# Block 1's RWKV-7 recurrence: products of one head on 64 or 32 partitions in place of masked products over 128

## The chip, the cores and the metric

The kernel runs on one core of a Trainium2 chip. The core has a matrix engine (TensorE, PE in the profile; PEld is its loading of weights), a vector engine (VectorE, DVE), a scalar engine (ScalarE, ACT), GpSimd (POOL), and SyncE (SP), which here only starts transfers. The metric is the device time of one execution in microseconds, the median of the runs; lower is better.

## The reference

Two transformer blocks over one sequence of 512 tokens with 1024 channels. In the first, half of the channels go through dilated attention and half through a bidirectional RWKV-7 mixer, then a product-key expert layer follows; the second block has a hybrid mixer and a mixture of experts. The change concerns the scan of RWKV-7, eight heads of 64 channels, in both directions:

```python
def wkv7_scan(r, w, k, v, kk, a, reverse):
    state0 = jnp.zeros((B, H, N, N), jnp.float32)
    def step(state, inp):
        r_t, w_t, k_t, v_t, kk_t, a_t = inp
        sa = jnp.einsum('bhvk,bhk->bhv', state, -kk_t)
        state = (state * w_t[:, :, None, :]
                 + sa[..., :, None] * (kk_t * a_t)[..., None, :]
                 + v_t[..., :, None] * k_t[..., None, :])
        y = jnp.einsum('bhvk,bhk->bhv', state, r_t)
        return state, y
    _, ys = lax.scan(step, state0, xs, reverse=reverse)
```

## The kernel before

The scan is computed in chunks: 512 tokens are eight chunks of 64, and a state is handed only from chunk to chunk. Two heads of 64 channels form a pair (four pairs, `j`), and a pair has two directions (`dr`). All of it is the function `rwkv`.

For each pair and direction, `elementwise` makes 128x512 operands with the channels of both heads on the partitions: `ar` (two of them), `x` (name `bx`), `y` (`kx`) and the decay `cum`. `by_head` makes from them `bd`: copies in which the other head's partitions are zeroed by the mask `own`, so that a product over all 128 partitions is that of one head. `within` transposes four operands to tokens-on-partitions (`transposed`, L611; the second direction's `vt` is instead turned by products with `flip`, L666), multiplies within each chunk (`pa` L694, then `pvy` and `pq`, L704 to L708, through masked `kbd`), and so gets the triangular matrices of each chunk. Tokens of two chunks lie on the 128 partitions here, so `vb` is again a masked copy.

`invert` and `solve` invert each chunk's triangular matrix: blocks of 16 by elimination, then blocks of 32 and 64 by small products, `p1` (L744 to L753) and `p2` (L764 to L770; the profile calls both `p`), whose operands `X`, `Z` (`Zb`), `V` (`Vb`) and `W` (`Wb`) are spread with zeros so that a product over 128 partitions is right. Then `pm` (L780), its two masked copies `M` (L783), and `pr`, `pq2` (L790 to L796) give per chunk `PB`, `RP` and `QQ`. `chain` walks the chunks: two sets of products into `pS` (L872, L875), four updates of the state `Sb` per chunk (L880), each of 64x64. `finish` normalises the pair's output (`mps`, L889).

The pairs are staged against each other: the loop over `j` does `forward` (`elementwise`, `within`) of pair `j` in the same turn as `backward` (`solve`), `invert`, `chain` and `finish` of pair `j - 1`. Between these, `fill` puts slices of the attention (`sps`, `ptps`, `po`) and of the modulation's products (`adaps`, L214, whose weights `adaw` stream in through two buffers of 512 KB). The recurrence is emitted at high priority. The order on each engine is set by the framework's scheduler from these priorities and its own estimate of times, not by the order of the text. After the last pair the output projection (`zps`) and the residual end block 1.

Of the kernel before, what the change touches and what calls it, by code (L numbers as in the profile page):

```python
# [40 lines left out]
def shape_consts():  # L41
# [15 lines left out]
    own = (p[:, None] // 64 == np.arange(2)[None, :]).astype(f)  # L57
    c["own"] = own
# [3 lines left out]
    i = np.arange(6)[None, :]  # L62
    c["m_b"] = np.concatenate([p[:, None] // 16 == np.arange(8), p[:, None] // 16 == i % 3 + 4 * (i // 3)], axis=1).astype(f)
    c["m_k"] = np.stack([r < q, r <= q], axis=1).astype(f)[:, :, None, :] * own[:, None, :, None]
# [14 lines left out]
    c["flip"] = np.eye(128, dtype=f)[::-1]  # L79
# [440 lines left out]
def rwkv(s, c, P, zrd, mixd, kkd, sad, gd, room, fill, tail):  # L520
# [23 lines left out]
    if True:  # L544
# [3 lines left out]
        gup = wp.tile([128, 512], F32, name="gup", tag="X", bufs=1)  # L548
        with tc.issue_after(s.ada_load.ins):
            own, m_nt, m_rb, m_e, m_b, m_k, id64, rst = [s.const(n, kp) for n in ("own", "m_nt", "m_rb", "m_e", "m_b", "m_k", "id64", "rst64")]  # L550
            for o, i in ((flip, A["k_flip"]), (lora, A["lora"]), (gup, A["g_up"])):
                nc.sync.dma_start(o, i)
# [8 lines left out]

        Zb = [kp.tile([128, 8, 2, 64], F32, name=f"Zb{d}") for d in range(2)]
        Vb = [kp.tile([128, 8, 4, 16], F32, name=f"Vb{d}") for d in range(2)]
        Wb = [kp.tile([128, 8, 2, 32], F32, name=f"Wb{d}") for d in range(2)]
        Sb = [kp.tile([128, 2, 2, 64], F32, name=f"Sb{d}") for d in range(2)]
        for t in Vb + Wb + Sb:
            nc.gpsimd.memset(t, 0.0)
# [49 lines left out]
        def elementwise(h, dr):  # L617
# [23 lines left out]
            x = wp.tile([128, 512], F32, name="bx", bufs=1)  # L641
            nc.gpsimd.tensor_tensor(x, rev(kkn), a, OP.mult)
            y = wp.tile([128, 512], F32, name="kx", bufs=1)
# [12 lines left out]

        def within(h, dr, ar, bd, x, y):
# [3 lines left out]
            if dr == 0:  # L661
                ps = transposed(h.zv)
            else:
                ps = P.tile([128, 4, 128], F32, name="tps", tag="tr")
                for tt in range(4):
                    mm(ps[:, tt, :], lhsT=flip, rhs=h.vt[:, 3 - tt, :], start=True, stop=True)  # L666
            h.vt = vt = wp.tile([128, 4, 128], F32, name="vt")
            nc.scalar.activation(vt, ps, AF.Copy)
            vb = wp.tile([128, 4, 2, 128], F32, name="vb", bufs=1)
            for cc in range(2):  # L670
                nc.scalar.activation(vb[:, :, cc, :], ps, AF.Copy, scale=own[:, cc:cc + 1])
            ta = wp.tile([128, 4, 2, 2, 64], F32, name="ta", bufs=3)
            ps = transposed(ar[:, 0, :])
            nc.scalar.activation(ta[:, :, :, 0, :], ps.rearrange("p a (e f) -> p a e f", e=2), AF.Copy)
            tb = wp.tile([128, 4, 2, 2, 64], F32, name="tb", bufs=3)
            ps = transposed(x)
            nc.scalar.activation(tb[:, :, :, 1, :], ps.rearrange("p a (e f) -> p a e f", e=2), AF.Copy)
            tk = wp.tile([128, 4, 128], F32, name="tk", bufs=1)
            ps = transposed(y)
            nc.scalar.activation(tk, ps, AF.Copy)  # L680
# [3 lines left out]
            for t2 in range(2):  # L684
                pv = P.tile([128, 2, 2, 2, 64], F32, name="pvy", tag="mm")
                pq = P.tile([128, 2, 2, 64], F32, name="pq", tag="mm")
                for ti in range(2):
                    tt = 2 * t2 + ti
# [7 lines left out]
                    nc.vector.tensor_tensor(db[:, 2 * tt:2 * tt + 2, :], pa[:, 0, :, 0, :], m_nt[:, None, :].to_broadcast([128, 2, 64]), OP.mult)  # L696
                    nc.vector.tensor_tensor(E[:, 2 * tt:2 * tt + 2, :], pa[:, 0, :, 0, :], m_e[:, None, :].to_broadcast([128, 2, 64]), OP.mult)
                    nc.vector.tensor_tensor(tb[:, tt, :, 0, :], pa[:, 0, :, 1, :], m_rb[:, None, :].to_broadcast([128, 2, 64]), OP.mult)
                    kb = wp.tile([128, 2, 2, 2, 64], F32, name="kbd")
                    for e in range(2):  # L700
                        nc.vector.tensor_tensor(kb[:, e], pa[:, 1, e, :, None, :].to_broadcast([128, 2, 2, 64]), m_k, OP.mult)
                    for cc in range(2):
                        for e in range(2):
                            mm(pv[64 * cc:64 * cc + 64, 0, ti, e, :], lhsT=kb[:, e, 0, cc, :], rhs=vt[:, tt, 64 * e:64 * e + 64], start=True, stop=True)  # L704
                    for e in range(2):
                        es = slice(64 * e, 64 * e + 64)
                        mm(pv[es, 1, ti, :, :], lhsT=vt[:, tt, es], rhs=kb[:, e, 1, :, :], start=True, stop=True)
                        mm(pq[es, ti, :, :], lhsT=tk[:, tt, es], rhs=vb[:, tt, :, es], start=True, stop=True)  # L708
                nc.scalar.activation(ta[:, 2 * t2:2 * t2 + 2, :, 1, :], pv[:, 0], AF.Copy)
                yv = yview(yacc, dr)[:, 256 * t2:256 * t2 + 256]  # L710
                py = pv[:, 1].rearrange("p a c t -> p (a c t)")
# [4 lines left out]
                nc.scalar.activation(QQ[:, dr, 4 * t2:4 * t2 + 4, :], pq.rearrange("p a c t -> p (a c) t"), AF.Copy)  # L716
# [9 lines left out]
        def solve(j, dr, held, zd, xd, QQ, PB, RP, y):  # L726
# [5 lines left out]
            for i, src in ((0, xd), (1, zd)):  # L732
                nc.sync.dma_start(zc[:, i], src[dr].rearrange("u g s t -> (g s) u t"))
            X = wp.tile([128, 8, 2, 3, 16], F32, name="X", bufs=1)
            nc.vector.tensor_tensor(X.rearrange("p u c q t -> p u (c q) t"), zc[:, 0, :, None, :].to_broadcast([128, 8, 6, 16]),
                                    m_b[:, None, 8:14, None].to_broadcast([128, 8, 6, 16]), OP.mult)
            nc.vector.tensor_tensor(Z.rearrange("p u c (q t) -> p u (c q) t", t=16), zc[:, 1, :, None, :].to_broadcast([128, 8, 8, 16]),
                                    m_b[:, None, 0:8, None].to_broadcast([128, 8, 8, 16]), OP.mult)

            p1 = P.tile([128, 3, 8, 16], F32, name="p1", tag="sv")  # L740
            for u in range(8):
                for g in range(4):
                    cc, h = g // 2, g % 2
                    mm(p1[32 * g:32 * g + 32, 0, u, :], lhsT=E[:, u, 32 * h:32 * h + 32], rhs=X[:, u, cc, 2 * h, :], start=True, stop=True)  # L744
            for g in range(4):
                po = slice(32 * g, 32 * g + 32)
                nc.scalar.activation(V[po, :, g, :], p1[po, 0], AF.Copy)
            for u in range(8):
                for g in range(4):
                    cc, h = g // 2, g % 2  # L750
                    mm(p1[32 * g:32 * g + 16, 1, u, :], lhsT=V[:, u, g, :], rhs=Z[:, u, cc, 32 * h + 16:32 * h + 32], start=True, stop=True)
                for cc in range(2):
                    mm(p1[64 * cc:64 * cc + 32, 2, u, :], lhsT=Z[:, u, cc, 0:32], rhs=V[:, u, 2 * cc, :], start=True, stop=True)  # L753
            for cc in range(2):
                po = slice(64 * cc, 64 * cc + 32)
                nc.vector.tensor_tensor(X[po, :, cc, 0, :], p1[po, 2], X[po, :, cc, 0, :], OP.add)
# [1430 lines left out]
```

## Time and profile before

| | |
|---|---|
| median of three runs | 2792.06 us (2790.89 to 2804.2) |
| profiled execution, its own time | 2790.26 us |
| its span, first to last instruction | 2788.5 us |
| mean granted TensorE clock | 0.961 |
| PE busy over the span | 2565.9 us (92%) |
| DVE, ACT, POOL busy | 1908.5, 1055.3, 1137.0 us |

Times are in microseconds from the span's start unless marked ns. "Busy" is time in which an engine executes; PE's weight loads lie beside its products. The recurrence's first product `pa` starts at 218 us, and block 1 ends at about 706 us; its output projection runs from 642 to 675 us with little else, and the chain of the last pair follows it, from 675 to 685 us. An f32 product on PE leaves two records, a transpose one. The tile of a product (as 128*64) is the rows and columns of the array that it uses; tiles of two column halves can run side by side.

### The profile page before, as it was taken

What the parts mean: (1) busy time and instruction counts of PE and PEld (TensorE: products, weight loads), DVE (VectorE), ACT (ScalarE), POOL (GpSimd) and SP (SyncE); (2) the same over time, 40 slices, a digit from 0 to 9 for tenths busy, and PEclk for the clock granted to TensorE, in tenths of its full rate; (3) what the DMA queues carried; (4) which work ended last, traced back from release to release, by engine and by line L of the source; (5) the groups of instructions that cost most, each with busy time, mean ns of one, the idle gap of its engine ahead of it and who ended that gap; (6) DMA issues with size and microseconds to landing.
All of it is one profiled execution on the core that took longest, in us unless ns stands there. A gap on an engine that the chain in (4) does not pass through costs nothing. (4 is left out here: it accounts for less than half of the span.)

```text
span 2788.5 us, 44586 instructions
## 1 busy us (share of the span) xinstructions
PE 2565.9 (92%) x16918; PEld 2037.5 (73%) x16918; DVE 1908.5 (68%) x3688; ACT 1055.3 (38%) x1973; POOL 1137.0 (41%) x864
## 2 busy tenths in 40 slices
PE   7999899978899997899999999999979999989995
PEld 4764455646789997899999999999967665654442
DVE  3666666743699888788888889888874377563323
ACT  3444344422434675233333333333333353222211
POOL 0012212111435766677767777776632123100002
PEclk9999999999999999999999999999989998889998
DMA  6527763371313678588888888886772212079984
GB/s 242 181 87 240 231 187 116 91 220 45 121 57 110 185 230 278 211 310 304 295 294 295 299 303 294 292 293 227 242 240 83 76 54 81 4 308 416 417 335 172
DMA packets 258888, 590.20 MB, mean 212 GB/s; under 512 B 48216, under 2 KB 121968, under 8 KB 248176
## 3 DMA queue, kind: packets, MB, share of 16 engines
q1 hardware_dynamic: 203584, 396.07, 41.1%
q0 software_dynamic: 38016, 138.43, 14.7%
q10 hardware_dynamic: 17072, 52.83, 5.1%
q8 instruction: 134, 2.20, 0.3%
q14 instruction: 82, 0.67, 0.1%
HBM read 530.23 MB, written 57.02 MB: 211 GB/s over the span
## 5 line engine op out<-in xcount | busy, mean ns | idle before, releaser
L165 PE MATMUL vacc<-gh,vhi 128*128 128x384 f32 x1024 | 347.0, 340 | 18.1 <-DVE xres L1359 9.9
L165 PE MATMUL ups<-phhi,uhi 128*128 128x384 f32 x1024 | 345.5, 338 | 6.0 <-ACT ge L1005 6.0
L167 PE MATMUL vacc<-gh,vlo 128*128 128x384 f32 x1024 | 324.0, 341 | 25.1 <-DVE vlo L171 20.0
L166 PE MATMUL ups<-phlo,uhi 128*128 128x384 f32 x1024 | 345.6, 338 | 1.3 <-DVE phlo L253 1.3
L166 PE MATMUL vacc<-gl,vhi 128*128 128x384 f32 x1024 | 346.0, 339 | 0.0
L167 PE MATMUL ups<-phhi,ulo 128*128 128x384 f32 x1024 | 345.4, 337 | 0.3 <-POOL ulo L171 0.3
L170 ACT ACTIVATE vhi<-vraw 128x512 fp32r<-128x512 f32 x256 | 161.0, 631 | 315.4 <-PE vacc L166 139.3
L171 POOL TENSOR_TENSOR vlo<-vraw,vhi 128x512 fp32r<-128x512 f32 x124 | 213.6, 1722 | 123.2 <-ACT vhi L170 105.3
L170 ACT ACTIVATE uhi<-uraw 128x1024 fp32r<-128x1024 f32 x128 | 135.6, 1060 | 284.8 <-PE ups L166 258.5
L1228 DVE SCALAR_TENSOR_TENSOR acc<-row,dot,acc 128x1024 f32<-128x1024 f32 x127 | 216.1, 1701 | 8.2 <-DMA row<-peer_v,peid 7.8
L167 PEld LDWEIGHTS vacc<-gh,vlo 128*128 128x128 f32 x1024 | 193.0, 192 | 30.5 <-DVE vlo L171 23.2
L165 PEld LDWEIGHTS vacc<-gh,vhi 128*128 128x128 f32 x1024 | 195.9, 192 | 20.8 <-DVE xres L1359 11.8
L1223 DVE CUSTOM_DVE_ANT_0 row<-row,phtok 128x1024 f32<-128x1024 f32 x128 | 195.1, 1525 | 10.7 <-DMA row<-u_rows,peid 10.7
L165 PEld LDWEIGHTS ups<-phhi,uhi 128*128 128x128 f32 x1024 | 193.5, 189 | 6.9 <-ACT ge L1005 6.7
L166 PEld LDWEIGHTS vacc<-gl,vhi 128*128 128x128 f32 x1024 | 195.8, 191 | 0.3
L166 PEld LDWEIGHTS ups<-phlo,uhi 128*128 128x128 f32 x1024 | 193.7, 189 | 1.7 <-DVE phlo L253 1.6
L167 PEld LDWEIGHTS ups<-phhi,ulo 128*128 128x128 f32 x1024 | 193.5, 189 | 0.9 <-POOL ulo L171 0.5
L1214 POOL DMA_INDIRECT row<-peer_v,peid x128 | 170.0, 1328 | 58.5 <-DVE acc L1228 33.4
L1214 POOL DMA_INDIRECT row<-u_rows,peid x128 | 167.7, 1311 | 50.8 <-DVE dot L1223 23.0
L171 DVE TENSOR_TENSOR vlo<-vraw,vhi 128x512 fp32r<-128x512 f32 x132 | 127.9, 970 | 73.5 <-ACT vhi L170 61.9
L1271 POOL TENSOR_TENSOR ge<-ge,wg 128x384 f32<-128x384 f32 x124 | 148.8, 1209 | 45.3 <-DMA wg<-wdr 31.7
L170 ACT ACTIVATE whi<-wraw 128x1024 fp32r<-128x1024 f32 (+1 forms) x81 | 84.7, 1046 | 209.4 <-PE zps L166 132.1
(655 smaller groups left out, 5719.0 us busy)
## 6 DMA issues: line engine op xcount, KB each, us to landing
uraw<-peer_u SPq DMA_DIRECT2D x128, 512.0 KB
vraw<-peer_v SPq DMA_DIRECT2D x256, 256.0 KB
wgu<-w_gu SPq DMA_DIRECT2D x32, 2048.0 KB
adaw<-ada_w SPq DMA_DIRECT2D x96, 512.0 KB
wdn<-w_dn SPq DMA_DIRECT2D x32, 1024.0 KB
wd<-wst SPq DMA_DIRECT2D x20, 1024.0 KB
wg<-wd ACTq DMA_DIRECT2D x16, 1280.0 KB
wraw<-w_in SPq DMA_DIRECT2D x22, 512.0 KB
```

Source lines behind the costliest of these rows:

```text
L165: mm(ps, lhsT=L[0], rhs=R[0], start=first, stop=False)
L166: mm(ps, lhsT=L[0], rhs=R[1], start=False, stop=False)
L167: mm(ps, lhsT=L[1], rhs=R[0], start=False, stop=last)
L170: s.nc.scalar.activation(hi, x, AF.Copy)
L171: return (eng or s.nc.vector).tensor_tensor(lo, x, hi.bitcast(F32), OP.subtract)
L1214: nc.gpsimd.indirect_dma_start(out=r, out_offset=None, in_=(urows, vrows)[which], in_offset=bass.IndirectOffsetOnAxis(ap=eid[:, p:p + 1], ...
L1223: nc.vector.tensor_tensor_reduce(out=r, in0=r, in1=htok, scale=1.0, scalar=0.0, op0=OP.mult, op1=OP.add, accum_out=dot[:, p:p + 1])
L1228: nc.vector.scalar_tensor_tensor(acc, r, dot[:, p:p + 1], acc, OP.mult, OP.add)
L1271: i = (nc.vector if grp == 0 and e % 2 == 0 else nc.gpsimd).tensor_tensor(g3, g3, W[0][:, :, e, :], OP.mult)
```

## The change

The same chunk of both heads now lies on the 128 partitions, in all stages of the recurrence: one head on rows 0 to 63 (`halves[0]`) and one on rows 64 to 127, or, where the matrices are inverted, four blocks of 32 (`quarters`). Every product is of one head alone, with its operands on 64 or 32 partitions and its result on the like. The masked copies `bd` and `vb`, the mask `own`, the second copy of `M`, the zeroed halves of `X`, `Z`, `V`, `W` and `Sb` and the `memset`s go. `x` and `y` are multiplied by `cum` on DVE, where POOL did it beside `bd`. `transposed` no longer uses PE's transpose of 128x128 but 16 ordinary f32 products of 64x64 with the identity as moving operand; `flip` turns within 64. The updates of `Sb` are two per chunk, over all 128 partitions.

```diff
         def transposed(src):
-            ps = P.tile([128, 4, 128], F32, name="tps", tag="tr")
-            for tt in range(4):
-                nc.tensor.transpose(ps[:, tt, :], src[:, 128 * tt:128 * tt + 128], s.ident)
+            ps = P.tile([128, 8, 64], F32, name="tps", tag="tr")
+            for ch in range(NCH):
+                for es in halves:
+                    mm(ps[es, ch, :], lhsT=src[es, 64 * ch:64 * ch + 64], rhs=s.ident[es, es], start=True, stop=True)
...
-            return ar, cum, x, y
-
-        def by_head(ar, cum, x, y):
-            bd = wp.tile([128, 2, 2, 512], F32, name="bd", bufs=1)
-            for i, z in ((0, x), (1, y)):
-                for e in range(2):
-                    nc.vector.scalar_tensor_tensor(bd[:, i, e, :], z, own[:, e:e + 1], cum, OP.mult, OP.mult)
-                nc.gpsimd.tensor_tensor(z, z, cum, OP.mult)
-            return ar, bd, x, y
+            nc.vector.tensor_tensor(x, x, cum, OP.mult)
+            nc.vector.tensor_tensor(y, y, cum, OP.mult)
+            return ar, x, y
...
-                    for i in range(2):
-                        for e in range(2):
-                            for cc in range(2):
-                                ch = 2 * tt + cc
-                                mm(pa[64 * cc:64 * cc + 64, i, e, :, :], lhsT=bd[:, i, e, 64 * ch:64 * ch + 64], rhs=ar[:, :, 64 * ch:64 * ch + 64],
-                                   start=True, stop=True)
+                    lo = 4 * t2 + 2 * ti
+                    for c in range(2):
+                        ts = slice(64 * (lo + c), 64 * (lo + c) + 64)
+                        for i, z in enumerate((x, y)):
+                            for es in halves:
+                                mm(pa[es, c, i, :, :], lhsT=z[es, ts], rhs=ar[es, :, ts], start=True, stop=True)
...
             for u in range(8):
-                for g in range(4):
-                    cc, h = g // 2, g % 2
-                    mm(p1[32 * g:32 * g + 16, 1, u, :], lhsT=V[:, u, g, :], rhs=Z[:, u, cc, 32 * h + 16:32 * h + 32], start=True, stop=True)
+                for g, gs in enumerate(quarters):
+                    h = g % 2
+                    mm(p1[32 * g:32 * g + 16, 1, u, :], lhsT=V[gs, u, :], rhs=Z[gs, u, 32 * h + 16:32 * h + 32], start=True, stop=True)
...
+            M = wp.tile([128, 8, 128], F32, name="M")
             for t2 in range(2):
...
-                M = wp.tile([128, 2, 2, 2, 128], F32, name="M")
-                for cc in range(2):
-                    nc.scalar.activation(M[:, :, :, cc, :], pm, AF.Copy, scale=own[:, cc:cc + 1])
+                nc.scalar.activation(M[:, cs], pm, AF.Copy)
...
                 if not last:
-                    for e in range(2):
-                        es = slice(64 * e, 64 * e + 64)
-                        for dr in range(2):
-                            nc.vector.scalar_tensor_tensor(Sn[es, dr, e, :], pS[es, 0, dr, :], GC[es, dr, ch:ch + 1], QQ[es, dr, ch, :], OP.mult, OP.add)
+                    for dr in range(2):
+                        nc.vector.scalar_tensor_tensor(Sn[:, dr, :], pS[:, 0, dr, :], GC[:, dr, ch:ch + 1], QQ[:, dr, ch, :], OP.mult, OP.add)
```

How this stands on PE, at two places. First, PE in the solve of pair 0's second direction, beside the forward products of pair 1's second direction; `p_...` is `p1`, and a row is a run of products with the shape of one. Before:

```order
L694 MATMUL pa<-ar,bd 64x128 x8
L704 MATMUL pvy<-vt,kbd 64x64 x3
L707 MATMUL pvy<-kbd,vt 64x128 x2
L751 MATMUL p_3052<-Zb_410,Vb_412 16x16 x4
L753 MATMUL p_3052<-Vb_412,Zb_410 32x16 x2
```

The changed program, at the same place:

```order
L736 MATMUL p_3233<-Vb_410,Zb_408 32x16 x2
L734 MATMUL p_3233<-Zb_408,Vb_410 16x16
L679 MATMUL pa<-ar,bx 64x128
L734 MATMUL p_3233<-Zb_408,Vb_410 16x16
L679 MATMUL pa<-ar,bx 64x128
L734 MATMUL p_3233<-Zb_408,Vb_410 16x16
L679 MATMUL pa<-ar,kx 64x128
L734 MATMUL p_3233<-Zb_408,Vb_410 16x16
L679 MATMUL pa<-ar,kx 64x128
L736 MATMUL p_3233<-Vb_410,Zb_408 32x16
```

Where eight `pa` stood together, single `pa` and single `p1` now alternate.

Second, PE in the second direction of pair 1, where its operands are transposed. Before:

```order
L780 MATMUL pm<-ta,Zb_409 64x128 x8
L214 MATMUL adaps<-adaw,crep_86 32x512 x2
L666 MATMUL tps<-vt,k_flip 128x128 x4
L611 MATMUL tps<-k_ident,ar 128x128 x4
L214 MATMUL adaps<-adaw,crep_86 32x512 x2
```

The changed program:

```order
L762 MATMUL pm<-ta,Zb_407 64x128 x8
L211 MATMUL adaps<-adaw,crep_86 32x512 x2
L657 MATMUL tps<-vt,k_flip 128x64 x8
L609 MATMUL tps<-k_ident,ar 64x64 x16
L769 MATMUL pr<-tb,M 64x128
L609 MATMUL tps<-k_ident,bx 64x64 x16
```

A set of four transposes has become one of 16 products, and a single `pr` now stands between two such sets.

## Rows read from the trace of the kernel before

**Rows 1.** Windows; columns: stretch, length, busy (x instructions), granted clock, DMA share, GB/s.

```profile
400.00:500.00 100.00, 86.89 (x1274) 55.32 (x1269) 67.27 (x209) 39.72 (x93) 20.25 (x17) 0.91 0.40 121
sum 506.00, PE 443.59 PEld 274.41 DVE 303.76 ACT 190.75 POOL 106.72; mean PE 88.72 PEld 54.88 DVE 60.75 ACT 38.15 POOL 21.34
```

**Rows 2.** Waits of PE, 200 to 706 us: us in total, times, longest.

```profile
PE adaps L214 <- DMA adaw<-ada_w: 31.0, 24, 3.5
PE lops L165 <- ACT mhi L170: 6.6, 1, 6.6
PE ptps L505 <- DVE pr L499: 5.2, 5, 3.1
PE pS L872 <- DVE Sb L880: 5.1, 9, 1.6
PE pa L694 <- DVE bd L653: 1.5, 4, 0.8
```

**Rows 3.** Groups by line, 200 to 706 us: xcount | busy us, mean ns | idle before.

```profile
L653 DVE SCALAR_TENSOR_TENSOR bd<-kx,k_own,cum 128x512 f32<-128x512 f32 x16 | 19.3, 1246 | 0.0
L653 DVE SCALAR_TENSOR_TENSOR bd<-bx,k_own,cum 128x512 f32<-128x512 f32 x16 | 12.5, 819 | 0.7 <-PE vps L167 0.7
L640 DVE TENSOR_TENSOR ar<-zr,ar 128x512 f32<-128x512 f32 x7 | 6.2, 892 | 1.0 <-ACT ar L637 1.0
L880 DVE SCALAR_TENSOR_TENSOR Sb<-pS,GC,QQ 64x64 f32<-64x64 f32 x96 | 23.0, 280 | 16.2 <-PE pS L875 15.5
L783 ACT ACTIVATE M<-pm,k_own 128x512 f32<-128x512 f32 x32 | 20.2, 684 | 30.7 <-PE pm L780 30.7
```

**Rows 4.** Timeline of PE: start us, us, what, xrecords, second turn's solve.

```profile
391.71 0.66 PE L790 MATMUL pr<-tb,M 128*64 128x128 f32 x8
392.20 0.39 PE L792 MATMUL pq<-M,tb 128*64 128x128 f32 x4
397.35 0.65 PE L611 MATMUL tps<-k_ident,bx 128*128 128x128 f32 x4
397.84 0.60 PE L611 MATMUL tps<-k_ident,kx 128*128 128x128 f32 x4
```

**Rows 5.** Timeline of PE, a long run of small products.

```profile
633.98 0.72 PE L744 MATMUL p<-X,E 128*32 128x16 f32 x56
```

**Rows 6.** Timeline of PE, single products of two shapes.

```profile
545.84 0.43 PE L694 MATMUL pa<-ar,bd 128*64 128x128 f32 x2
546.21 0.21 PE L751 MATMUL p<-Zb,Vb 128*16 128x16 f32 x2
546.35 0.43 PE L694 MATMUL pa<-ar,bd 128*64 128x128 f32 x2
```

**Rows 7.** Timeline of PE, the same beside `p2`.

```profile
557.90 0.33 PE L704 MATMUL pvy<-vt,kbd 128*64 128x64 f32 x2
558.16 0.26 PE L770 MATMUL p<-Zb,Wb 128*32 128x32 f32 x4
558.34 0.34 PE L704 MATMUL pvy<-vt,kbd 128*64 128x64 f32 x4
```

**Rows 8.** Timeline of PE, the last pair's chain.

```profile
674.97 0.46 PE L872 MATMUL pS<-Sb,PB 128*64 128x64 f32 x8
675.25 0.45 PE L875 MATMUL pS<-RP,Sb 128*64 128x64 f32 x8
676.07 0.99 PE L872 MATMUL pS<-Sb,PB 128*64 128x64 f32 x7 [0.37 <-DVE Sb L880]
677.72 0.99 PE L872 MATMUL pS<-Sb,PB 128*64 128x64 f32 x7 [0.37 <-DVE Sb L880]
```

**Rows 9.** Timeline of DVE, the last pair's chain.

```profile
675.75 0.99 DVE L880 SCALAR_TENSOR_TENSOR Sb<-pS,GC,QQ 64x64 f32<-64x64 f32 x4
```

**Rows 10.** Timeline of PE, block 2, two row halves.

```profile
2320.77 0.27 PE L1738 MATMUL gp<-SD,V 64*64 64x64 f32 x1
2320.78 0.27 PE L1742 MATMUL gp<-SD,V 64*64 64x64 f32 x1
```

More of the change, by code (lines that the diff above doesn't have):

```diff
@@ L560, in rwkv @@
         nc.vector.tensor_scalar(hwa, s.v("w0", 0, 16), 0.5, None, OP.mult)
[L562 to L567, printed above, removed]
+        Zb = [kp.tile([128, 8, 64], F32, name=f"Zb{d}") for d in range(2)]
+        Vb = [kp.tile([128, 8, 16], F32, name=f"Vb{d}") for d in range(2)]
+        Wb = [kp.tile([128, 8, 32], F32, name=f"Wb{d}") for d in range(2)]
+        Sb = [kp.tile([128, 2, 64], F32, name=f"Sb{d}") for d in range(2)]
+        halves = [slice(0, 64), slice(64, 128)]
+        quarters = [slice(32 * g, 32 * g + 32) for g in range(4)]
         def c64(x):
@@ L663, in within @@
             else:
[L664 to L667, printed above, removed]
+                ps = P.tile([128, 8, 64], F32, name="tps", tag="tr")
+                for ch in range(NCH):
+                    mm(ps[:, ch, :], lhsT=flip, rhs=h.vt[:, 7 - ch, :], start=True, stop=True)
+            h.vt = vt = wp.tile([128, 8, 64], F32, name="vt")
             nc.scalar.activation(vt, ps, AF.Copy)
-            vb = wp.tile([128, 4, 2, 128], F32, name="vb", bufs=1)
-            for cc in range(2):
[L671 to L680, printed above, removed]
+            ta = wp.tile([128, 8, 2, 64], F32, name="ta", bufs=3)
+            nc.scalar.activation(ta[:, :, 0, :], transposed(ar[:, 0, :]), AF.Copy)
+            tb = wp.tile([128, 8, 2, 64], F32, name="tb", bufs=3)
+            nc.scalar.activation(tb[:, :, 1, :], transposed(x), AF.Copy)
+            tk = wp.tile([128, 8, 64], F32, name="tk", bufs=1)
+            nc.scalar.activation(tk, transposed(y), AF.Copy)
             db = wp.tile([128, 8, 64], F32, name="db", bufs=1)
@@ new lines, in within @@
+                    for c in range(2):
+                        for es in halves:
+                            mm(pq[es, 2 * ti + c, :], lhsT=tk[es, lo + c, :], rhs=vt[es, lo + c, :], start=True, stop=True)
+                    for c in range(2):
+                        for es in halves:
+                            mm(pv[es, 0, 2 * ti + c, :], lhsT=kb[es, c, 0, :], rhs=vt[es, lo + c, :], start=True, stop=True)
+                    for c in range(2):
+                        for es in halves:
+                            mm(pv[es, 1, 2 * ti + c, :], lhsT=vt[es, lo + c, :], rhs=kb[es, c, 1, :], start=True, stop=True)
@@ L733, in solve @@
                 nc.sync.dma_start(zc[:, i], src[dr].rearrange("u g s t -> (g s) u t"))
[L734 to L738, printed above, removed]
+            X = wp.tile([128, 8, 3, 16], F32, name="X", bufs=2)
@@ L754, in solve @@
-            for cc in range(2):
-                po = slice(64 * cc, 64 * cc + 32)
-                nc.vector.tensor_tensor(X[po, :, cc, 0, :], p1[po, 2], X[po, :, cc, 0, :], OP.add)
-            for g in range(4):
-                po = slice(32 * g, 32 * g + 16)
-                nc.scalar.activation(Z[po, :, g // 2, 32 * (g % 2) + 16:32 * (g % 2) + 32], p1[po, 1], AF.Copy)
+                for g, gs in enumerate(quarters):
+                    h = g % 2
+                    mm(p1[gs, 0, u, :], lhsT=E[gs, u, 32 * h:32 * h + 32], rhs=X[gs, u, 2 * h, :], start=True, stop=True)
@@ new lines, in solve @@
+            nc.scalar.activation(V, p1[:, 0], AF.Copy)
+            for u in range(8):
+                for g, gs in enumerate(quarters):
+                    h = g % 2
+                    mm(p1[32 * g:32 * g + 16, 1, u, :], lhsT=V[gs, u, :], rhs=Z[gs, u, 32 * h + 16:32 * h + 32], start=True, stop=True)
+                for gs in quarters[::2]:
+                    mm(p1[gs, 2, u, :], lhsT=Z[gs, u, 0:32], rhs=V[gs, u, :], start=True, stop=True)
+            for gs in quarters[::2]:
+                nc.vector.tensor_tensor(X[gs, :, 0, :], p1[gs, 2], X[gs, :, 0, :], OP.add)
@@ new lines, in solve @@
+                    lo, hi = quarters[2 * cc:2 * cc + 2]
+                    mm(p2[lo, 1, u, :], lhsT=W[hi, u, :], rhs=Z[hi, u, 32:64], start=True, stop=True)
+            for lo in quarters[::2]:
+                nc.scalar.activation(Z[lo, :, 32:64], p2[lo, 1], AF.Copy)
+            M = wp.tile([128, 8, 128], F32, name="M")
+            for t2 in range(2):
+                cs = slice(4 * t2, 4 * t2 + 4)
+                pm = P.tile([128, 4, 128], F32, name="pm", tag="sv")
+                for c in range(4):
+                    for es in halves:
+                        mm(pm[es, c, :], lhsT=Z[es, 4 * t2 + c, :], rhs=ta[es, 4 * t2 + c, :, :], start=True, stop=True)
+                nc.scalar.activation(M[:, cs], pm, AF.Copy)
+                pr = P.tile([128, 4, 2, 64], F32, name="pr", tag="sv")
+                pq = P.tile([128, 2, 4, 64], F32, name="pq2", tag="sv")
+                for c in range(4):
+                    u = 4 * t2 + c
+                    for es in halves:
+                        mm(pr[es, c, :, :], lhsT=M[es, u, 0:64], rhs=tb[es, u, :, :], start=True, stop=True)
+                for c in range(4):
+                    u = 4 * t2 + c
+                    for es in halves:
+                        mm(pq[es, 0, c, :], lhsT=tb[es, u, 1, :], rhs=M[es, u, 64:128], start=True, stop=True)
+                    for es in halves:
+                        mm(pq[es, 1, c, :], lhsT=M[es, u, 64:128], rhs=tb[es, u, 0, :], start=True, stop=True)
+                nc.vector.tensor_tensor(RP[:, dr, cs, :], pr[:, :, 0, :], c64(ar[:, 1, :])[:, cs, :], OP.add)
+                nc.vector.tensor_tensor(PB[:, dr, cs, :], pr[:, :, 1, :], id64[:, None, :].to_broadcast([128, 4, 64]), OP.add)
+                nc.vector.tensor_tensor(QQ[:, dr, cs, :], pq[:, 0], QQ[:, dr, cs, :], OP.add)
@@ L801, in solve @@
                 yv = yview(y, dr)[:, 256 * t2:256 * t2 + 256]
[L802 removed]
+                nc.vector.tensor_tensor(yv, pq[:, 1].rearrange("p c t -> p (c t)"), yv, OP.add)
         class Pair:
```

124 lines of the change are left out of this document (39 added, 85 removed).

## Prediction

> **What bounds the kernel now.** The order of the two programs comes first, since it says which part of the span can move at all: on PE everything from the output projection's tail on (the last 9470 products) stands in the same order before and after. So only the stage from about 218 us (the first `pa` product) to about 706 us can change, and the 2084 us behind it cost the same, shifted.
>
> In that stage I read the windows first. PE is busy 443.59 of 506 us, DVE 303.76, ACT 190.75, POOL 106.72 [rows 1]: PE bounds it, with 506 − 443.59 = 62.4 us idle. The waits of PE say what ends this idle time [rows 2]: 31.0 us, in 24 pieces, are `adaps` waiting for the `adaw` load, which the change doesn't touch; 6.6 us are one wait of `lops` behind the stage's tail; only the rest, 62.4 − 31.0 − 6.6 = 24.8 us, is spread over waits for DVE, ACT and issue inside attention and the recurrence. Then the groups by line give the durations of what goes away [rows 3], and the PE timeline the price of a product in a run and alone [rows 4 to 7].
>
> **The change part by part.**
>
> *Vector engines.* DVE loses 32 `bd` products, 19.3 + 12.5 = 31.8 us, and gets 16 plain products of 128x512; by the `ar` product that is 16 × 0.892 = 14.3 us. 48 of the 96 `Sb` updates go: I take the longer ones at the same 0.280, so 13.4 us [rows 3]. X and Z are built at half size. So DVE loses at least 31.8 − 14.3 + 13.4 = 31 us. ACT loses half of the 32 copies of `M`, 10.1 us [rows 3], and the 16 copies `vb`; POOL loses its 16 products by `cum`. None of these bounds the stage, so none of it counts by itself; it counts where PE waits for it. Those waits are the 24.8 us above. `pa` on `bd` (1.5 us) goes entirely, `pS` on `Sb` (5.1) halves, `ptps` on `pr` (5.2), which is attention's softmax queued behind the recurrence on DVE, should shrink with a shorter DVE queue [rows 2]. Bounds: 0 (the next operand is late instead) and −22 (2.2 of the 24.8 belong to the last chain below). I take a bit under half, **−9 us**: about half of the named waits lies behind operands that stay.
>
> *The last chain.* The chain of pair 3 (675 to 685 us) has nothing beside it: a step lasts 677.72 − 676.07 = 1.65 us [rows 8], of which four `Sb` updates take 0.99 [rows 9]. Two updates take 0.50, so six steps lose 0.49 each: **−3 us**. The chains of the other pairs lie beside attention and ada products. Bounds: −4 and +1 (each of the longer updates as long as two).
>
> *Transposes.* PE has 28 sets of four transposes through the identity; each becomes a set of 16 f32 products of 64x64. A set of four lasts 397.84 − 397.35 = 0.49 us [rows 4]. A product of 128 columns: eight records (an f32 product leaves two) of `pr` last 392.20 − 391.71 = 0.49 us, two column halves side by side, so 0.12 per product [rows 4]; with 64 columns eight records of `pS` last 0.28 us, 0.07 per product, with the change of tile in it, so I take 0.06 for a long run [rows 8]. 16 products at 0.06 are 0.96 us, 0.47 more than now: 28 × 0.47 = **+13 us**. Bounds: 0 and, if the two halves don't run side by side, 28 × (1.92 − 0.49) = +40.
>
> *Everything else on PE keeps its columns.* `pa`, `pm`, `pr`, `pq`, `p1`, `p2` contract over 64 or 32 rows where they contracted over 128, but move as many columns as before, and the rows show that it is columns that cost (0.49 us for the eight records of 128, 0.28 for those of 64). A product that skips zero rows gains nothing for PE.
>
> *Order.* What does change is how the small products of the solve stand among the others. Before, a run of `pa` of a pair's two column halves alternates with short runs of `p1`; after, single products alternate with single products, as the first pair of order listings shows. Counted over the whole order, products that stand alone between products of another tile shape go from 3 to 41 for `pa`, 4 to 61 for `p1`, 0 to 21 for `p2`, 9 to 25 for `pvy` and 0 to 21 for `pq`. What one costs alone, from the few that stand so before: `pa` 546.21 − 545.84 = 0.37 us, `p1` 546.35 − 546.21 = 0.14 us [rows 6]; `pvy` 558.16 − 557.90 = 0.26 us; two `p2` products 558.34 − 558.16 = 0.18 us [rows 7], for one 0.16. In a run they cost 0.12, 0.03 (28 products of `p` in 0.72 us [rows 5]), 0.07 and 0.03. So: `pa` 38 × 0.25 = 9.5; `p1` 57 × 0.11 = 6.3; `pvy` and `pq` 37 × 0.19 = 7.0; `p2` 21 × 0.13 = 2.7: **+26 us**. Bounds: 0, if tiles of 64 and 32 rows can follow one another without the gap that the rows show for 128-row tiles, and +34, if a third more is lost at short runs that aren't single.
>
> *What the `adaw` loads swallow.* PE's 31.0 us of waits for `adaw` are waits for a stream: where PE comes later to the product, the wait is shorter. +39 us of PE work stand against that, spread over the 488 us, while the 24 waits lie in 24 places. What is added at a place counts only up to the wait that follows, and what is late by then is late for good. Bounds 0 and −31; I take a third, **−10 us**.
>
> Sum: −9 − 3 + 13 + 26 − 10 = +17. On the profiled execution's 2790.3 us (span 2788.5) that is 2807; on the median of the runs, 2792.06, it is 2809. I say **2808 us**.
>
> **The rivals.**
>
> *B, the work is swallowed.* The same +39, but 25 of it disappear in the `adaw` waits and 12 in the vector engines' waits: 39 − 25 − 12 − 3 = −1, so 2785 to 2795. For it: the waits are there, 24 of them. Against: the waits average 1.3 us and the longest is 3.5, while the additions cluster at the solves.
>
> *C, faster.* Changes between 64- and 32-row tiles cost nothing, so +26 falls to about 0, and the waits on DVE and ACT go: 13 − 18 − 3 − 10 = −18, 2772 us. For it: DVE loses a tenth of its work, ACT too. Against: single products show a gap at each change of shape, whichever shapes follow [rows 6, 7].
>
> *D, slower.* The changed kernel puts the two row halves' products next to each other into one accumulation buffer (`pa[es, ...]` and so on), where before two column halves shared 128 rows. If such two don't run side by side, every product that doesn't stand alone costs what two cost together now: by the order, 471 products of 128 columns 0.12 us more each (+57), 802 of 64 columns 0.06 more (+48), and the 448 that transpose 0.06 more (+27), +132 in all. With 35 of it swallowed by the waits for `adaw` and `ptps` that are still left, this is 2807 + 97, about 2905 (2880 to 2930). It decides from the point where half of the pairs stand apart. For it: no row of before shows two row halves with one buffer. Against: of two row halves with different buffers the starts lie 2320.78 − 2320.77 = 0.01 us apart [rows 10], so the halves as such run side by side.
> The Trainium skill, "TensorEngine Tiling (Array Packing)", section "Restrictions and Gotchas", says under PSUM pressure that different row tiles go to different PSUM banks and can't use the same bank at the same time. By that rule, D's time would come; the rows with different buffers agree with it, and no run here shows the case of one bank.
>
> **How the numbers follow.** The forecast has 0.50, B 0.17, C 0.16, D 0.17. The forecast's own range is 2793 (19 swallowed, 14 of the waits gone) to 2840 (nothing swallowed, no wait gone, and a granted clock of 0.90 in place of about 0.95, which on 443.59 us of PE work is 24 us; a window of 0.91 is in [rows 1]). For 8 in 10 I leave out D (0.17) and a few hundredths beyond C: 2762 to 2850.
> A measurement of this kernel tells 0.5% from no change: 2778.1 to 2806.0 is the same. Faster: 0.14 of C and 0.02 of B, 0.16. The same: 0.15 of B, 0.17 of the forecast, 0.02 of C, 0.34. Slower: 0.33 of the forecast and D's 0.17, 0.50.
>
> **What would show it.** Right: the 16-fold `tps` groups last about 0.96 us a set, single `pa` between `p` products 0.37, the last chain's step 1.15, DVE's busy time in the stage is 31 us or more lower, PE's busy time some 30 us higher, the `adaw` waits near 21 us. Two products of one pair that start 0.1 us apart instead of 0.01 make it D; `adaw` waits under 8 us make it B; single `pa` at 0.15 make it C. A window with a granted clock far from 0.95 in this stage would make all of the sum wrong by more than any of its terms.

## The result and the profile after

The changed kernel takes 2886.46 us, median of four runs (2885.3 to 2895.3); the kernel before, beside it, 2791.8. The ratio is 1.0335 (1.03 to 1.0371): slower by 95 us, where 2808 had been forecast.

The first view is one window over the stage, from the first `pa` to the first `lops`: stretch, length, busy time (and instructions) of PE, PEld, DVE, ACT and POOL, granted clock, DMA share, GB/s. The kernel before:

```profile
218.30:696.10 477.80, 416.61 (x5273) 254.37 (x5273) 285.15 (x818) 181.53 (x403) 100.15 (x79) 0.95 0.53 165
```

The changed kernel, the same work:

```profile
224.90:794.30 569.40, 499.19 (x6418) 316.00 (x6417) 239.32 (x714) 157.49 (x348) 75.17 (x61) 0.85 0.44 137
```

All of the loss lies here. DVE lost 46 us of work, ACT 24, POOL 25, and none of it came back as time, for PE grew by 83. The granted clock says why the prediction's terms can't explain this: 0.95 has become 0.85. The changed kernel's windows that answer to [rows 1] show it in the middle of the stage:

```profile
400.00:500.00 100.00, 82.19 (x1095) 50.29 (x1094) 39.25 (x129) 24.00 (x56) 9.71 (x9) 0.86 0.48 148
500.00:600.00 100.00, 92.76 (x1279) 67.30 (x1280) 49.28 (x165) 28.49 (x68) 7.58 (x8) 0.73 0.16 40
```

From 500 to 600 us PE is busier than in any other 100 us of the stage, at a clock of 0.73, and DMA moves 40 GB/s: PE hardly waits there, it is slow.

Its timeline on PE (start us, us, what) shows one fall of the clock, at 512.4 us, from its full level (2.4 GHz) to its lower one (1.2 GHz):

```profile
511.16 0.43 PE L679 MATMUL pa<-ar,kx 64*64 64x128 f32 x2
511.52 0.23 PE L736 MATMUL p<-Vb,Zb 32*32 32x16 f32 x2
511.68 0.43 PE L679 MATMUL pa<-ar,bx 64*64 64x128 f32 x2
512.04 0.23 PE L736 MATMUL p<-Vb,Zb 32*32 32x16 f32 x2
512.20 0.51 PE L679 MATMUL pa<-ar,bx 64*64 64x128 f32 x2
512.64 0.23 PE L734 MATMUL p<-Zb,Vb 32*16 32x16 f32 x2
512.80 0.69 PE L679 MATMUL pa<-ar,kx 64*64 64x128 f32 x2
513.41 0.23 PE L734 MATMUL p<-Zb,Vb 32*16 32x16 f32 x2
```

Single products alternate at the price that was forecast, 511.68 − 511.16 = 0.52 us a couple, as in [rows 6]. Then the same `pa` lasts 0.69 instead of 0.43, and goes on so until 539.7 us, through dense work too.

To split the loss I added up, for each PE record of the stage, the time to the next record's start without idle time, apart for full and half clock. "Work" is the full part plus half of the half-clock part: about what the same records would take at full clock.

| us | first `pa` at | full clock | half clock | work | idle |
|---|---|---|---|---|---|
| before | 218.3 | 379.6 | 37.0 | 398.1 | 61.2 |
| changed | 224.9 | 348.0 | 151.2 | 423.6 | 70.2 |

So 98 us later at the stage's end are: 57 from the clock, (151.2 − 37.0) / 2; 25.5 more work; 9 more idle; 6.6 before the first `pa`. The spans differ by 97.2. The half is a little too much for single products: the step of a single `pa` above goes from 0.36 us (511.52 − 511.16) to 0.61 (513.41 − 512.80), not to 0.72. They have 26.8 of the 151.2 us, so some 3 of the 57 us are rather work.

What stood before each fall of the clock sorts the 57 us. All eight falls in the stage of the kernel before, and ten of the sixteen in the changed kernel's, come behind waiting: PE idled 1.4 to 3.1 us in the 5 us ahead of them. The other six (at 379.3, 474.9, 512.4, 580.7, 621.6 and 635.3 us) come with at most 0.13 us idle, and ahead of each single products alternate: `pa` with `p` three times, `pa` with the turns by `flip` once, `pvy` or `pq` with `p` twice. The stretches that these six begin have 94.8 of the 151.2 us, 47 us of loss; those behind waits have 56.4, where the kernel before has 37.0 in all. One fall of each kind (the 5 us ahead of it, columns as above), first the kernel before's at 403.3, then the changed kernel's at 512.4:

```profile
398.30:403.30 5.00, 2.52 (x24) 1.31 (x22) 3.74 (x8) 1.43 (x3) 2.97 (x2) 1.00 0.92 209
507.40:512.40 5.00, 4.87 (x104) 3.53 (x96) 3.98 (x14) 0.81 (x2) 0.00 (x0) 1.00 0.25 69
```

The waits of PE that answer to [rows 2] (us in total, times, longest):

```profile
PE adaps L211 <- DMA adaw<-ada_w: 31.6, 30, 3.0
PE lops L162 <- ACT mhi L167: 6.6, 1, 6.6
PE pS L848 <- DVE Sb L842: 6.2, 3, 2.3
PE ptps L502 <- DVE pr L496: 4.5, 6, 2.2
PE pS L848 <- DVE Sb L854: 4.3, 9, 0.9
```

The groups that answer to [rows 3] (xcount | busy us, mean ns | idle before):

```profile
L854 DVE SCALAR_TENSOR_TENSOR Sb<-pS,GC,QQ 128x64 f32<-128x64 f32 x48 | 11.4, 279 | 22.3 <-PE pS L851 22.3
L763 ACT ACTIVATE M<-pm 128x512 f32<-128x512 f32 x16 | 9.5, 594 | 29.9 <-PE pm L762 29.9
L644 DVE TENSOR_TENSOR bx<-bx,cum 128x512 f32<-128x512 f32 x6 | 5.0, 840 | 0.0
```

The vector engines' prices were near the estimates (279 ns for a longer update, 840 for a product by `cum`, estimated from `ar` at 892). They bound nothing in the stage, but ahead of it the products by `cum`, now on DVE, stand in front of `vA`, the sum that empties the accumulation buffer of PE's `vps`. DVE, and then PE:

```profile
207.73 0.68 DVE L644 TENSOR_TENSOR bx<-bx,cum 128x512 f32<-128x512 f32 x1
208.34 0.68 DVE L645 TENSOR_TENSOR kx<-kx,cum 128x512 f32<-128x512 f32 x1
208.94 0.68 DVE L437 TENSOR_TENSOR vA<-vps,vA 128x512 f32<-128x512 f32 x1
```

```profile
209.67 0.79 PE L162 MATMUL vps<-whi,hhi 128*128 128x512 f32 x1 [3.60 <-DVE vA L437]
```

PE waits 3.6 us, and runs at half clock from 208.6 to 215.5 us; the kernel before has neither (its two waits for `vA` are 0.4 us together). That is most of the 6.6 us before the first `pa`.

Two long runs, in the changed kernel's timeline of PE. Transposes answer to [rows 4]:

```profile
502.01 1.15 PE L609 MATMUL tps<-k_ident,kx 64*64 64x64 f32 x32
502.99 0.28 PE L769 MATMUL pr<-tb,M 64*64 64x128 f32 x2
```

A set lasts 0.98 us (0.96 was taken). And `pa` in a run:

```profile
332.10 0.39 PE L679 MATMUL pa<-ar,bx 64*64 64x128 f32 x4
332.32 0.39 PE L679 MATMUL pa<-ar,kx 64*64 64x128 f32 x4
```

Two products (four records) take 0.22 us: the halves do run side by side in one buffer.

The last chain answers to [rows 8, 9]. PE and then DVE:

```profile
773.41 0.69 PE L848 MATMUL pS<-Sb,PB 64*64 64x64 f32 x8 [0.38 <-DVE Sb L854]
773.89 0.64 PE L851 MATMUL pS<-RP,Sb 64*64 64x64 f32 x8
```

```profile
773.07 0.48 DVE L854 SCALAR_TENSOR_TENSOR Sb<-pS,GC,QQ 128x64 f32<-128x64 f32 x2 [1.31 <-PE pS L851]
774.58 0.48 DVE L854 SCALAR_TENSOR_TENSOR Sb<-pS,GC,QQ 128x64 f32<-128x64 f32 x2 [0.77 <-PE pS L851]
```

The updates halved to 0.48 us, but a step lasts 774.58 − 773.07 = 1.51 us instead of 1.65: these products run at half clock, which began at 771.8 us behind a wait of 2.0 us for the copy of the first state (`Sb` L842).

### The profile page after: what moved, and what is told of

Its sections match the earlier page's. It is cut to its first block, busy times and chain, and to the rows that moved or that the text cites. A ratio compares the mean times of both kernels' runs of the same rounds, so it can differ in the third digit from the quotient of the medians.

```text
span 2885.7 us, 46792 instructions
## 1 busy us (share of the span) xinstructions
PE 2657.6 (92%) x18118; PEld 2104.0 (73%) x18118; DVE 1875.2 (65%) x3588; ACT 1029.1 (36%) x1917; POOL 1117.3 (39%) x842
## 5 line engine op out<-in xcount | busy, mean ns | idle before, releaser
L1200 DVE SCALAR_TENSOR_TENSOR acc<-row,dot,acc 128x1024 f32<-128x1024 f32 x127 | 207.3, 1632 | 11.6 <-DMA row<-peer_v,peid 10.0
L168 DVE TENSOR_TENSOR vlo<-vraw,vhi 128x512 fp32r<-128x512 f32 x132 | 136.7, 1036 | 65.1 <-ACT vhi L167 56.7
```

The lines of the kernel that those rows point to most:

```text
L168: return (eng or s.nc.vector).tensor_tensor(lo, x, hi.bitcast(F32), OP.subtract)
L1200: nc.vector.scalar_tensor_tensor(acc, r, dot[:, p:p + 1], acc, OP.mult, OP.add)
```

## The experiments

**First round: is it the order or the tiles?**

`pin` and `before_pin` put an order on PE:

```diff
+        turn = lambda: tc.issue_after(newest[0].ins)
...
-                    backward(prev, 0)
+                    with turn():
+                        backward(prev, 0)
```

(and so for `forward(cur, 1, ew)` and `backward(prev, 1)`; `newest` is the recurrence's last product).

> The changed kernel, with one edit: the solve of a pair is issued on TensorE behind the last product of the forward work emitted before it, and the second forward behind the solve before it, so that single pa and p1 products no longer alternate (the order has no pa, pvy, pq or p1 standing alone, against 41, 25, 21 and 61). Theory 1, alternation: products that stand alone keep TensorE occupied but do little, and the granted clock falls behind them; without them the lost work (about 25 us) and most of the low clock (151 us of PE time at half clock against 37 before) go: 2795 to 2820 us, mean granted clock over the span 0.955 or more, clock in 500 to 600 us 0.9 or more. Theory 2, the tiles: products on 64x64 tiles load only half of the array, so the clock falls with them in whatever order they stand: clock stays at 0.94 over the span, and only the 25 us go, 2855 to 2870 us.

> The kernel before with the same edit of the order as pin. Its order has few single products to lose (3 pa, 4 p1). Theory 1: nothing to win, 2785 to 2800 us, clock 0.96. Theory 3, that pinning is worth something by itself (attention fills the waits better): 2770 us or less.

`pin`: 2868.34 us, 1.0304 (1.0256 to 1.0352). `before_pin`: 2852.28, 1.0234 (1.019 to 1.0278), a loss that nothing had expected. The edit isn't neutral: PE idles 107.4 us in `before_pin`'s stage where it idled 61.2. `pin` fitted theory 2 by its time, but by another way: its work fell to 395.1 us, below the kernel before's, idle rose to 103.0, and 125.1 us were at half clock. An order that makes PE wait can't tell the theories apart. `pin` against `before_pin`, alike in order, is only 16 us apart.

`pin_tps2` does the transposing products twice.

> pin with every transposing product through the identity done twice (448 more products of 64x64). The prediction's term: a set of 16 lasts 0.96 us, so 28 sets add 27 us to pin by themselves if nothing swallows them. Theory 1: pin plus 20 to 27 us and no change of the clock, since they stand in runs of 16. Theory 2: the clock falls further, pin plus 35 us or more.

2936.06 us, 68 more than `pin`: by the time alone theory 2's range (35 or more), though not by its way. In the profiled executions, 58 us apart, the stage is 44 us longer: work rose by 421.1 − 395.1 = 26 us, as the term said, idle by 12.6, and PE time at half clock by 10, which costs 5. The other 15 us lie behind the stage, where the same products take 2080.6 to 2102.6 us in the profiled executions of this document's kernels. So the size of the term stands, and it is not swallowed; why idle grew beside it is open.

`micro` is TensorE by itself:

> TensorE alone, six stretches of products without waits, each behind 12 products of 128x128 with 512 columns. It computes nothing of the reference. (A) 320 products on diagonal 64x64 tiles, 128 columns, one accumulation buffer; (B) 320 on 128x64 tiles as in the kernel before; (C) 560 on 64x64 tiles with 64 columns; (D) 80 times one of A and one 32x32 product of 16 columns; (E) the same with 128x64 and 128x32 tiles; (F) 20 times eight of A and 32 of the 32x32 ones. Theory 1: clock 1.0 in A, B, C and F, 0.5 in D and E alike, at 0.5 us a couple. Theory 2: 0.5 in A, C, D and F, 1.0 in B and E. Rival D of the prediction (row halves in one buffer don't run side by side): A takes twice B's time at the same clock.

Windows of A, B, C, D and E; columns as before, PE busy first and the granted clock the third from the end:

```profile
32.00:67.00 35.00, 35.00 (x641) 34.83 (x641) 0.00 (x0) 0.00 (x0) 1.00 0.01 2
77.50:112.50 35.00, 35.00 (x641) 34.90 (x640) 0.00 (x0) 0.00 (x0) 1.00 0.01 2
123.00:156.00 33.00, 33.00 (x1122) 32.86 (x1122) 0.00 (x0) 0.00 (x0) 1.00 0.01 4
166.40:231.00 64.60, 64.60 (x323) 36.12 (x323) 0.00 (x0) 0.00 (x0) 0.53 0.00 1
242.00:284.00 42.00, 42.00 (x313) 25.67 (x312) 0.00 (x0) 0.00 (x0) 1.00 0.00 1
```

A and B take the same 35 us for 320 products, so rival D is out. Runs on 64x64 tiles keep the full clock (A, C). Alternation on small tiles (D) loses it 4 us after its start and for all the rest of the stretch; alternation on 128 rows (E), at the same 0.52 us a couple, keeps it. Neither theory had that: it takes the tiles and the alternation together. F kept it too, but for two pieces of 3.4 us; PE waited 7.6 us for instructions there.

**Second round: the order by priority.**

`solve_first` takes the alternation away without a wait; `forward_first` gives the forward work the priority, `before_solve_first` edits the kernel before as `solve_first` does:

```diff
+        more = lambda: tc.high_priority(offset=300)
...
-                    backward(prev, 0)
+                    with more():
+                        backward(prev, 0)
```

> The changed kernel with one edit: the solve of a pair is emitted at 300 more priority, so that its products and the forward ones no longer have equal priority and no longer alternate one by one (single pa, pvy, pq and p1 products fall from 41, 25, 21 and 61 to 2, 0, 0 and 0), and TensorE is not made to wait for it as in pin. Theory 1, alternation of products on few rows lets the clock fall: 2795 to 2825 us, PE time at half clock 40 to 70 us against 151 of the changed kernel. Theory 2, the smaller tiles lower the clock wherever they stand among waits: 2845 to 2875 us, 110 us or more at half clock.

> As solve_first, but the forward work has the 300 more (single products 0 pa, 0 pvy, 2 pq, 2 p1). Both theories as there; the two should agree within 20 us if what counts is only that the single products are gone.

> The kernel before with the edit of solve_first. Its products don't alternate, so theory 1 expects 2780 to 2800 us. If the solve's place by itself helps or hurts, it moves by more than 15 us and solve_first has to be read against it: the difference of the two is then the price of the change without alternation, 15 to 30 us by theory 1 (transposes +13 us, and some clock), 60 or more by theory 2.

| | us | ratio | full clock | half clock | work | idle |
|---|---|---|---|---|---|---|
| `solve_first` | 2820.21 | 1.0129 (1.0095 to 1.0162) | 351.7 | 82.7 | 393.0 | 67.8 |
| `forward_first` | 2857.02 | 1.0248 (1.0227 to 1.0269) | 365.5 | 75.5 | 403.2 | 92.9 |
| `before_solve_first` | 2785.88 | 0.9984 (0.9966 to 1.0001) | 365.2 | 53.6 | 392.0 | 59.3 |

Each split is of the one execution that was profiled: 2809.77, 2853.22 and 2792.05 us long, and 2887.57 for the changed kernel. `solve_first` wins back 66 of the 95 us, and 67 at the stage's end: 30.6 of work and 34 of clock, (151.2 − 82.7) / 2. That is theory 1's range, and its time at half clock is a little above the 40 to 70 expected. All of its 13 falls of the clock come behind waiting (0.8 us or more in the 5 us ahead); none of the kind without waiting is left. `forward_first` has as little alternation and no more time at half clock, but 25 us more idle (8.6 of it `pvy` behind `kbd`) and 10 more work: that the two would agree was wrong, and its time lies in theory 2's range without theory 2's half clock. The priority alone does nothing to the kernel before, so the change without alternation costs 34 us, just above theory 1's 15 to 30: 32 at the stage's end, of which 15 clock, 8.5 idle, 8 a later first `pa`, 1 work. The stage window of `solve_first`:

```profile
225.20:727.40 502.20, 434.41 (x6418) 278.15 (x6417) 241.60 (x714) 157.18 (x348) 79.03 (x61) 0.89 0.49 156
```

`micro2` asks which products do it:

> TensorE alone, as micro; it computes nothing of the reference. Three stretches of 80 couples: (G) a 64x64 product of 64 columns and a 32x32 one of 16, (H) a 64x64 one of 128 columns and a 128x32 one, (I) a 128x64 one and a 32x32 one. Then four times 40 couples as in D of micro (which fell to half clock) with, behind them, a run of (J) 240 products on 64x64 tiles of 128 columns, (K) 240 on 128x64 tiles, (L) 400 on 64x64 tiles of 64 columns, (M) 800 on 32x32 tiles. If rows in use times columns count, G falls, H falls, I stays at full clock, and after the couples K comes back to full clock within 7 us and M does not; J and L may take longer than K. If only the gaps between products count, G to I all fall (E of micro already speaks against that) and J to M all come back alike.

Windows of G, H and I, and of the four runs behind the couples, J to M:

```profile
31.00:77.70 46.70, 46.70 (x321) 35.00 (x320) 0.00 (x0) 0.00 (x0) 0.55 0.00 1
91.10:154.00 62.90, 62.90 (x320) 35.52 (x320) 0.00 (x0) 0.00 (x0) 0.55 0.00 1
166.80:208.50 41.70, 41.70 (x320) 25.77 (x320) 0.00 (x0) 0.00 (x0) 1.00 0.00 1
249.00:278.00 29.00, 29.00 (x484) 28.60 (x483) 0.00 (x0) 0.00 (x0) 0.91 0.01 2
318.00:347.00 29.00, 29.00 (x485) 28.20 (x486) 0.00 (x0) 0.00 (x0) 0.92 0.01 2
386.00:412.00 26.00, 26.00 (x796) 25.23 (x798) 0.00 (x0) 0.00 (x0) 0.91 0.02 4
452.00:495.00 43.00, 24.41 (x1607) 22.94 (x1606) 0.00 (x0) 0.00 (x0) 0.50 0.02 4
```

G and H fall, I doesn't. Runs of the 64x64 or 128x64 products bring the clock back alike (0.91, 0.92, 0.91); the run of 32x32 products never does, though it also stood idle for 18.6 of its 43 us, so that this one is not clean.

**Third round: the same inside the kernel.**

`after_bd` has the masked copies back, for `pa` alone:

```diff
-                        for i, z in enumerate((x, y)):
-                            for es in halves:
-                                mm(pa[es, c, i, :, :], lhsT=z[es, ts], rhs=ar[es, :, ts], start=True, stop=True)
+                        for i in range(2):
+                            for e, es in enumerate(halves):
+                                mm(pa[es, c, i, :, :], lhsT=bd[:, i, e, ts], rhs=ar[:, :, ts], start=True, stop=True)
```

> The changed kernel with the masked copies bd back for pa alone: pa contracts again over 128 rows (with zeros for the other head), everything else is as changed, the equal priorities too, so that single products still alternate (31 pa, 37 pvy, 22 pq, 67 p1, 24 p2). DVE has 17 us more to do. Theory after the runs on TensorE alone: the clock falls where products on 64 rows alternate with small ones and not where those on 128 rows do, at the same time a couple. So PE time at half clock falls from 151 us to 80 to 125 (pvy and pq still stand on 64 rows), and the time to 2835 to 2870 us. Rival, the gaps between the products alone: no change of the clock, 2880 to 2900 us.

2891.06 us, 1.0376 (1.0341 to 1.0411): the time is outside the expectation and in the rival's range. The 130.3 us at half clock, also outside it, are those of the profiled execution, the fastest of five (2874.76 us at a mean clock of 0.945; the others have 0.937 to 0.941, the changed kernel 0.938 to 0.944). So the totals show no gain in clock. Windows around one of its falls:

```profile
478.00:483.00 5.00, 4.48 (x64) 3.33 (x52) 2.33 (x6) 0.12 (x1) 0.00 (x0) 1.00 0.01 3
483.00:507.00 24.00, 24.00 (x206) 15.83 (x204) 4.53 (x16) 3.80 (x11) 0.00 (x0) 0.50 0.06 15
```

In the first of them its `pvy` products of 64 columns alternate with `p`, as in G; the `pa` that follow inherit the half clock (25.0 us of `pa` at half clock, 22.3 in the changed kernel). All four falls without waiting in `after_bd` (at most 0.52 us idle in the 5 us ahead) come behind `pq` and `pvy` that alternate with `p` on 64 rows as before; at 483 us two single `pa` stand last. In the changed kernel the three longest of them came behind `pa` and `p`. The third of these, at 580.7 us, and the same stretch in `after_bd`, whose clock falls 3.4 us later behind `pq` and `pvy`:

```profile
576.20:580.70 4.50, 4.50 (x50) 2.84 (x50) 3.01 (x8) 0.00 (x0) 2.72 (x2) 1.00 0.05 10
580.70:601.20 20.50, 20.50 (x192) 14.07 (x188) 5.65 (x19) 5.48 (x15) 1.17 (x2) 0.50 0.16 45
```

```profile
563.60:568.40 4.80, 4.80 (x58) 3.12 (x56) 3.31 (x9) 0.00 (x0) 2.72 (x2) 1.00 0.19 35
```

So single `pa` on 128 rows start no fall here. What begins behind alternation falls from 94.8 to 54.8 us, but falls behind waits have 75.5 where they had 56.4, and work and idle rise by 11: the time gains nothing.

`before_alternating` is the counterpart, the kernel before made to alternate (`offset=35` in place of 300):

> The kernel before with the solve at 35 more priority, which makes its solve and forward products alternate one by one as the changed kernel's do (single products 38 pa, 14 pvy, 2 pq, 37 p1, 10 p2, about 100 in all; before has about 20, the changed kernel 169). All of them contract over 128 rows. Theory after the runs on TensorE alone, alternation costs work in any kernel but the clock only where the products use few rows: PE work at full clock 10 to 20 us more than before, PE time at half clock 25 to 60 us (before 37), 2798 to 2818 us. Rival, the gaps of alternation alone let the clock fall: 80 us or more at half clock, 2825 to 2850 us.

2815.59 us, 1.0128 (1.0067 to 1.0188), in the range; 66.5 us at half clock (in the fastest of its runs, 2806.79 us), a little above it, and work up by 6.3, below it. 15.9 of the 66.5 are `pS`, and of `pa`, `p` and `pvy` together 12.7 us are at half clock, where the changed kernel has 56. Three of its stretches, the first right behind a fall, the others with `pa` and `p` alternating:

```profile
362.80:376.50 13.70, 13.70 (x92) 7.67 (x93) 2.04 (x9) 2.87 (x8) 0.00 (x0) 0.50 0.10 32
377.00:381.00 4.00, 4.00 (x40) 2.40 (x39) 0.42 (x1) 0.32 (x1) 0.00 (x0) 1.00 0.73 255
573.00:577.50 4.50, 4.50 (x36) 2.76 (x35) 0.00 (x0) 0.00 (x0) 0.00 (x0) 1.00 0.60 208
```

In the second and third, and in a fourth at 474 us, `pa` of 128 columns on 128 rows alternate with `p`, and the clock holds. The first, the only one of its nine falls without waiting, fell behind `pvy` of 64 columns on 128 rows, which "few rows" doesn't explain. `micro3` asked that:

> TensorE alone, as micro; it computes nothing of the reference. Stretches of couples: (N) 80 times a 128x64 product of 64 columns and a 128x32 one of 16; (O) 80 times a 128x64 one of 64 columns and a 32x32 one. Then 64x64 products of 128 columns and 32x32 ones in groups: (P) 2 and 2, 60 times; (Q) 4 and 4, 40 times; (R) 8 and 8, 30 times. If rows alone decide, N and O stay at full clock, and before_alternating fell at 362 us for another reason. If rows and columns count together, N and O fall as that stretch did, although E and I with 128 columns did not. For the groups, whose time a product falls with their size: P falls too, R stays at full clock, Q is open.

Windows of N, O, P, Q and R:

```profile
31.00:78.60 47.60, 47.60 (x320) 35.92 (x320) 0.00 (x0) 0.00 (x0) 0.55 0.00 1
91.60:138.40 46.80, 46.80 (x321) 35.18 (x320) 0.00 (x0) 0.00 (x0) 0.56 0.00 1
150.50:182.40 31.90, 31.90 (x481) 19.94 (x480) 0.00 (x0) 0.00 (x0) 1.00 0.01 2
193.00:223.40 30.40, 30.40 (x637) 22.44 (x638) 0.00 (x0) 0.00 (x0) 1.00 0.01 2
234.00:271.90 37.90, 37.90 (x961) 31.89 (x960) 0.00 (x0) 0.00 (x0) 1.00 0.01 3
```

N and O fall, so rows alone don't decide. And P, two and two, already holds, as Q and R do: 240 products in 32 us where D's 160 took 63.

**The part that could be kept.** `before_chain` is the kernel before with the changed `chain` alone, `before_chain_sf` that with `solve_first`'s priority.

> The kernel before with only the chain changed as in the changed kernel (pS products of one head on 64 rows, two updates of Sb per chunk). The prediction's term: -3 us at the last chain, and 13 us less on DVE off the path, 2784 to 2790 us where before has 2791. Theory of the clock: pS products on 64 rows between waits let the clock fall in the last chain and behind it, which takes back 2 to 6 us: 2788 to 2797.

> before_chain with the solve at 300 more priority, the best parts found so far together. before_solve_first was 0.9984 of before (interval to 1.0001): expected 2775 to 2790 us, below before by 0.1 to 0.5%.

2787.53 us, 1.0003 (0.9981 to 1.0024), and 2789.6, 1.0014 (0.9995 to 1.0033): no change by either. The kernel before took 2786.52 us beside them, not the 2791 that the ranges were reckoned from: taken as differences, +1 us is in the range of the clock's theory (−3 to +6) and not in the prediction's term (−7 to −1), though an interval of 6 us to either side tells little, and the second is not below before as expected. No version here beats the kernel before clear of noise.

## Why the prediction was wrong

- *Transposes, +13:* right. Their work went from 15.0 to 26.8 us, and `pin_tps2` gives 26 for as many again. Missed beside it: the turns by `flip`, for each of four pairs 4 products of 128 columns before and 8 of 64 now, went from 4.1 to 8.5 us of work in all. "Everything else on PE keeps its columns" was wrong there: half the columns did not halve the time of a product over the whole array. It was wrong the other way for `pS`, whose work fell from 24.0 to 15.3 us with the new chain (16.1 in `before_chain`).
- *Order, +26:* near in size (30.6 us of work went with the alternation), and wrong as a price. A single product was charged its own 0.37 or 0.14 us. What it does to the products behind it, by the clock, was 34 us more in the same experiment.
- *The clock* is the step that failed. The sum kept the mean of 0.95, and the range's upper end took 0.90 (24 us) as the worst. Measured: 0.85, 57 us, 47 of them in stretches that begin behind alternating single products. The prediction's last sign, a clock far from 0.95, is the one that came. Its upper end is also added up wrongly: 2790 + 39 − 3 + 24 is 2850, not 2840, and 2886 lies above both. The rows that the prediction had, singles on 128 rows at full clock [rows 6], could not show it, and the changed tiles were taken to be equal to them because a run takes equal time.
- *The `adaw` waits, −10:* wrong. 31.6 us in 30 pieces stand where 31.0 stood [rows 2]. *Waits on DVE and ACT, −9:* wrong; idle time rose by 9, and `pS` alone waits 6.2 us for the copy of the first state (L842), 0.3 before. That DVE's work counts only where PE waits for it was right; that the moved products by `cum` would make PE wait, ahead of the first `pa`, was missed. In `after_bd`, where POOL makes them again, PE doesn't wait for `vA`, and the first `pa` starts at 219.3 us.
- *The last chain, −3:* the updates halved as said, but half clock left a step at 1.51 us where 1.15 was forecast: −0.8.
- *Rivals:* D had the right range (2880 to 2930) for the wrong reason. Side by side in one buffer is what `micro` A and the `pa` runs show; the rule of the Trainium skill's "TensorEngine Tiling (Array Packing)", "Restrictions and Gotchas", by which one bank would exclude it, does not hold for these diagonal tiles. B and C failed with the waits.

Shown: the loss is at PE, 57 of 98 us by the clock, and two thirds of the loss goes with the alternation. Open: what holds the other 34 us together behind the 8 us before the first `pa`, and why the clock stays low through dense work such as from 524 to 539 us. Alternation with every product on 128 rows and 128 columns was tried on TensorE alone and, for `pa`, in single stretches of kernels, not for the whole changed kernel. The change also gives `X`, `bx` and `kx` a second buffer and `kbd` a third, and puts `pq` before `pvy`; no run takes these apart.

## What to carry to other kernels

Judge a smaller tile not by a long run, where it cost nothing here, but by how its products will stand among others: ask the program's order how many stand alone, and price the clock beside the gap. Where two strands of work have equal priority, give one the precedence and check which, since the other way round cost 37 us. An engine that is not the bound can lose 46 us of work and give nothing back, and two products moved to it can stand in front of what the bound waits for. And before calling a low clock a matter of waiting, look at whether the engine idled ahead of the fall: six falls here came without.

## What the hardware showed unexpectedly

With PE busy 64.60 of 64.60 us by its records, the granted clock was 0.53. Alternating single products lost the full clock with 64x64 and 32x32 tiles (D, G), with 64x64 and 128x32 (H), and with 128x64 products of 64 columns between 128x32 or 32x32 ones (N, O). They kept it with 128x64 products of 128 columns between 128x32 or 32x32 ones (E, I); so did groups of two and more of 64x64 and 32x32 (P, Q, R). In the kernels, three stretches of single `pa` on 64x64 tiles with `p` lost it, and four on 128x64 tiles kept it. Behind a fall, 64x64 products in a run brought it back in 4.5 us (from 249.6 to 254.1 in `micro2`).
